# Sums of weight quarters on VectorE alone, and filters in half the steps

## The chip, the cores and the metric

The kernel runs on one core of one Trainium2 chip. It is one layer of a diffusion transformer in fp32, launched once. The metric is the device time of a launch in microseconds (us). Five engines work side by side: TensorE (PE: matrix products), VectorE (DVE), ScalarE (ACT), GpSimd (POOL) and SyncE (SP), which issues most of the DMAs. Each engine carries out its own instructions in the order of its own queue.

## The reference, cut to what matters

```python
def swiglu(x, wg, wu, wd):
    return (jax.nn.silu(x @ wg) * (x @ wu)) @ wd

def half_ffn(h, shift, scale, gate, wg, wu, wd):
    return h + 0.5 * gate * swiglu(modulate(rms_norm(h), shift, scale), wg, wu, wd)

def hyena_kernels(l, w1, b1, fr1, w2, b2, fr2, w3):
    t, z = hyena_pos_features(l)
    h = jnp.sin(fr1 * (z @ w1 + b1))
    h = jnp.sin(fr2 * (h @ w2 + b2))
    h = (h @ w3).astype(jnp.float32).reshape(l, HYENA_ORDER, 2, B_WIDTH)
    ...
    window = jnp.exp(-t[:, None] * deltas[None, :]) + HYENA_SHIFT
    h = h * window[:, None, None, :]
    kern = jnp.concatenate([h[:, :, 0], jnp.flip(h[:, :, 1], axis=0)], axis=0)
    return kern / (jnp.sum(jnp.abs(kern), axis=0, keepdims=True) + HYENA_L1_EPS)

def reference(x, c, ctx, ...):
    m = jnp.split((jax.nn.silu(c) @ mod_w[l] + mod_b[l])[:, None, :], N_MOD, axis=-1)
    ...
    h = half_ffn(h, m[0], m[1], m[2], ffn_w_gate[l, 0], ffn_w_up[l, 0], ffn_w_down[l, 0])
    hc = half_ffn(hc, mc[0], mc[1], mc[2], ffn_w_gate[l, 0], ffn_w_up[l, 0], ffn_w_down[l, 0])
    ...                    # norms, then the mixers: four gated recurrent heads and a Hyena convolution
    out, _, _ = token_mixers(n, s_fw, s_bw, hyena_kernels(n_lat, *filt_w), *mix_w)
    h = h + m[5] * out
    h = half_ffn(h, m[6], m[7], m[8], ffn_w_gate[l, 1], ffn_w_up[l, 1], ffn_w_down[l, 1])
    return rms_norm(h) * final_norm_w
```

The model width is 1024, with 512 tokens in `h`, 256 in the context `hc`, and 2816 hidden units (22 tiles of 128). The change lies in the first `half_ffn` and in `hyena_kernels`.

## The kernel before

Every fp32 product is made of three products of rounded parts. `split` (L141) casts a tile to its high part on ScalarE (L142) and subtracts that from the tile for the low part on VectorE or GpSimd (L143); `mm3` (L312) then issues the three products (L314, L315, L317).

The first feed-forward block treats 512 + 256 tokens and goes through the 22 hidden tiles in five groups: `GROUPS0` is 0-4, 4-8, 8-12, 12-16 and 16-22. Group 0 is made plainly. In the others (below: groups 1 to 4; the first three have four pairs of weight tiles, the last has six) two neighbouring tiles of `wg`, or of `wu`, are multiplied together in `pair_products0` (L869) by the seven products of the Strassen-Winograd scheme. With a pair's weight quarters a11, a12 (from the first tile, `src0`) and a21, a22 (from the second, `src1`), the seven left operands are p1: a11, p6: s2 = a11 + a21 + a22, p7: s3 = a11 + a21, p5: s1 = a21 + a22, p2: a12, p4: a22, p3: s4 = a12 + s2 (the weights are stored with the signs that make all of these additions). Each product is 12 matmuls of 386 columns. After each group but the last there follow the "down" products with `wd`; their sums go to DRAM through accumulating DMAs on GpSimd's queue (`y_dram`, `yc_dram`).

`quads0` (L239) prepares a pair's operands, one with each `yield`. a11, a12 and a22 are loaded as quarters into tiles `wraw`. s1 and s3 are made in tiles `qs` by two DMAs each: one of SyncE loads a quarter, one of GpSimd (L247) adds the other quarter to it. s2 and s4 are sums of VectorE (L254). a11, a12 and a22 are split with the subtraction on GpSimd, the others with VectorE. The ring of `wraw` tiles has three buffers of 128x1024, that of the split weights three as well; `weights(3)` keeps up to four or five operands ahead.

Between the products, `adv(bg)` moves on a background of other work: `mod_steps` (L393) loads a 128x1024 tile `wmod` of the modulation weights per step, into one of two buffers, and VectorE multiplies it by the conditioning vector and sums it up (L390: two `junk` products and one `wmod` product per tile for the first tiles, one for the later ones).

After the block come the residual and norms, then the input projections (`w_in`), beside which `filters` (L721) makes the Hyena filters in four passes (two channel halves, two orders). A pass is a generator whose `yield` hands a pair of estimated costs (TensorE, VectorE) to the class `Clock`, which decides when the next step is issued, and fills the time between steps with weight products. A pass has these steps: loads of the last weights `w3r` and of the first window (a decay table `win`); the weights' split into `w3h` and `w3l`; four steps, each with two taps products, the windowed product `hw` (L761) on VectorE, its sum and difference `pm` on GpSimd, and the next window's load; the norm; its reciprocal; six steps of the spectrum (`ps_k`). So twelve `yield`s follow the first two. The windows and `w3h`, `w3l` are tiles of the class `c2` (14 buffers of 512 columns).

The tiles `res` (`quarters`, two buffers of 128x2x770) hold the results of the pair products and, later, the gates of the recurrent heads (work items "z" of the table `todo`, L171). One weight of the last group's down products is kept there as well (`RES2`, L159); `ONE8` is a tile of another class, of 2080 columns, with twelve buffers.

What sets the order: the program is written as straight code with generators; a scheduler then places instructions on each engine's queue by a timeline of its own. SyncE's queue is in order: a load that waits for its buffer holds up the loads behind it.

## Time and profile before

| | |
|---|---|
| median of 3 runs | 1643.78 us (1643.22 to 1647.12) |
| profiled execution | 1642.22 us, span 1640.4 us, mean granted clock 0.953 |
| TensorE busy | 1489.6 us (91%) |
| VectorE busy | 1151.7 us (70%) |
| ScalarE, GpSimd busy | 631.7 us (39%), 467.8 us (29%) |
| groups 1 to 4 of the first block | 148.6-226.4, 259.9-347.8, 381.3-469.1, 502.5-621.3 us |
| the down products between them | 33.4 to 33.5 us each |
| filters, beside the norms and projections | from about 626 to 900 us |

The times are from one profiled execution, counted from the start of its span. A stretch in which TensorE is busy all the time at full clock (1.00, 2.4 GHz) has no room but by having less to multiply; a stretch with idle TensorE or a lower granted clock (0.5 is 1.2 GHz) does. The shares of the whole span average over stages that differ much, so the stretches are read one by one.

### The profile page before, as it was taken

The numbers are of one execution on the slowest core, as the hardware profiler recorded it, in microseconds if no ns is written. First come the engines' busy times: TensorE is split into PE (matmuls) and PEld (weight loads), VectorE is DVE, ScalarE is ACT, GpSimd is POOL, SyncE is SP. The second block draws the span as 40 slices with busy tenths as digits, with TensorE's granted clock in tenths as the row PEclk, the third lists the DMA queues.
The fourth block names the chain that finished last, engine by engine and source line by source line (L and its number), as shares of the span: only waits on it lengthen the run. The fifth ranks groups of instructions, "written<-read, shape, count | busy, mean of one in ns | idle before, by whom it ended". The sixth has DMA issues, their size and how long they took to land.

```text
span 1640.4 us, 22788 instructions
## 1 busy us (share of the span) xinstructions
PE 1489.6 (91%) x8560; PEld 1328.0 (81%) x8560; DVE 1151.7 (70%) x1811; ACT 631.7 (39%) x1133; POOL 467.8 (29%) x380
## 2 busy tenths in 40 slices
PE   8798897896896999989999998998789999999997
PEld 5687886886886887867778887887679899989897
DVE  7785784674774667866646986867566767969687
ACT  5253332332332443434323342344433443525353
POOL 1021443534534541332565001211332011202120
PEclk9899998998998999989999998999989999999999
DMA  9217559558568348243543443113343123333322
GB/s 388 88 59 247 164 151 233 141 151 224 145 170 204 90 107 307 81 147 110 170 150 105 135 167 135 65 52 116 103 149 110 50 73 109 104 103 96 112 76 91
DMA packets 95055, 224.57 MB, mean 137 GB/s; under 512 B 10651, under 2 KB 23711, under 8 KB 94304
## 3 DMA queue, kind: packets, MB, share of 16 engines
q1 hardware_dynamic: 79920, 198.69, 36.4%
q0 software_dynamic: 13440, 23.21, 8.0%
q8 instruction: 67, 1.10, 0.3%
q10 hardware_dynamic: 1584, 1.20, 0.2%
q14 instruction: 44, 0.36, 0.1%
HBM read 190.83 MB, written 32.24 MB: 136 GB/s over the span
## 4 chain that ended last, share of the span: by engine, by line
PE 60%; DMA 14%; DVE 12%; issue 7%; POOL 4%; ACT 3%; SPq 1%; ACTq 0%; POOLq 0%; DVEq 0%
DMA qs<-in_wg 5%; PE ps_w L314 5%; PE ps_w L317 5%; PE ps_w L315 5%; PE ps_dl L314 4%; PE ps_p L314 4%; PE ps_p L317 4%; PE ps_dl L317 4%; PE ps_p L315 4%; PE ps_dl L315 4%; DMA wmod<-in_mod_w 4%; DMA qs<-in_wu 3%; DVE wlo L143 2%; PE ps_s L1370 1%; PE ps_gl L314 1%
## 5 line engine op out<-in xcount | busy, mean ns | idle before, releaser
L142 ACT CAST whi<-wraw 128x512 fp32r<-128x512 f32 (+2 forms) x191 | 154.5, 810 | 273.5 <-issue 72.3
L143 DVE TENSOR_TENSOR wlo<-wraw,whi 128x1024 fp32r<-128x1024 f32 (+2 forms) x118 | 126.8, 1077 | 61.5 <-ACT whi L142 57.4
L317 PE MATMUL ps_w<-nhi,wlo 128*128 128x512 f32 x352 | 141.3, 402 | 6.8 <-DVE wlo L143 6.8
L314 PE MATMUL ps_w<-nhi,whi 128*128 128x512 f32 x352 | 144.5, 411 | 0.0
L315 PE MATMUL ps_w<-nlo,whi 128*128 128x512 f32 x352 | 141.0, 401 | 0.0
L317 PE MATMUL ps_dl<-mid,wlo 128*128 128x512 f32 (+1 forms) x330 | 128.4, 391 | 0.0
L315 PE MATMUL ps_dl<-mid,whi 128*128 128x512 f32 (+1 forms) x330 | 128.1, 389 | 0.0
L314 PE MATMUL ps_dl<-mid,whi 128*128 128x512 f32 (+1 forms) x330 | 126.8, 392 | 0.0
L143 POOL TENSOR_TENSOR wlo<-wraw,whi 128x1024 fp32r<-128x1024 f32 x19 | 47.2, 2485 | 248.4 <-ACT whi L142 244.2
L1570 POOL TENSOR_TENSOR u<-p,res 128x512 f32<-128x512 f32 x18 | 32.9, 1828 | 284.4 <-ACT p L1565 140.6
L390 DVE SCALAR_TENSOR_TENSOR wmod<-wmod,cvb 128x1024 f32<-128x1024 f32 x56 | 79.2, 1416 | 19.5 <-DMA wmod<-in_mod_w 19.1
L142 ACT CAST wlo<-qs 128x512 fp32r<-128x512 f32 x72 | 43.5, 618 | 113.1 <-DMA qs<-in_wu 45.1
L317 PEld LDWEIGHTS ps_w<-nhi,wlo 128*128 128x128 f32 x352 | 67.8, 193 | 20.7 <-DVE wlo L143 7.7
L314 PE MATMUL ps_p<-tt,wlo 128*128 128x386 f32 x72 | 31.1, 431 | 55.2 <-ACT wlo L142 55.2
L314 PEld LDWEIGHTS ps_w<-nhi,whi 128*128 128x128 f32 x352 | 68.1, 193 | 15.3
L142 ACT CAST whi<-qs 128x512 fp32r<-128x512 f32 x72 | 43.8, 619 | 93.8 <-DMA qs<-in_wg 34.9
L315 PEld LDWEIGHTS ps_w<-nlo,whi 128*128 128x128 f32 x352 | 68.2, 194 | 11.7
L143 DVE TENSOR_TENSOR wlo<-qs,wlo 128x512 fp32r<-128x512 f32 x72 | 63.1, 882 | 14.1 <-ACT wlo L142 13.8
L314 PEld LDWEIGHTS ps_dl<-mid,whi 128*128 128x128 f32 x330 | 62.5, 190 | 12.8 <-ACT mid L142 0.2
L254 DVE TENSOR_TENSOR qs<-qs,wraw 128x512 f32<-128x512 f32 x18 | 14.3, 796 | 82.1 <-DMA qs<-in_wg 61.9
L317 PEld LDWEIGHTS ps_dl<-mid,wlo 128*128 128x128 f32 x330 | 62.9, 191 | 8.2 <-DVE wlo L143 0.2
L315 PEld LDWEIGHTS ps_dl<-mid,whi 128*128 128x128 f32 x330 | 62.7, 190 | 7.9
(531 smaller groups left out, 4956.0 us busy)
## 6 DMA issues: line engine op xcount, KB each, us to landing
wmod<-in_mod_w SPq DMA_DIRECT2D x56, 512.0 KB, 4.0
wraw<-in_w_in SPq DMA_DIRECT2D x44, 512.0 KB, 3.5
wraw<-in_wd SPq DMA_DIRECT2D x37, 384.0 KB, 3.4
wraw<-in_wg SPq DMA_DIRECT2D x26, 512.0 KB, 4.0
wraw<-in_wu SPq DMA_DIRECT2D x26, 512.0 KB, 3.5
wraw<-in_wd SPq DMA_DIRECT2D x40, 256.0 KB, 3.0
wm<-in_mod_w SPq DMA_DIRECT2D x16, 512.0 KB, 10.0
wraw<-in_wg SPq DMA_DIRECT2D x27, 256.0 KB, 5.0
```

Source lines behind the costliest of these rows:

```text
L142: A.copy(hi, x)
L143: return eng.tensor_tensor(out=lo, in0=x, in1=hi.bitcast(F32), op=ALU.subtract)
L254: V.tensor_tensor(out=t, in0=x, in1=y, op=ALU.add)
L314: PE.matmul(o, whi, xhi, start=first, stop=False)
L315: PE.matmul(o, whi, xlo, start=False, stop=False)
L317: PE.matmul(o, wlo, xhi, start=False, stop=last)
L390: return V.scalar_tensor_tensor(out=out_, in0=raw, scalar=1.0, in1=vec, op0=ALU.mult, op1=ALU.mult, accum_out=res)
L1370: PE.matmul(p_[:, ss], km[:, ss], view(QA, c * P, ([2 * b, P // (2 * b)], [L + b, 2], [1, b])), start=True, stop=True)
L1570: G.tensor_tensor(out=u57, in0=p57, in1=res[:, 1:2].broadcast_to([P, 2, 256]), op=ALU.add)
```

## The change

Three things change. In `quads0` both tiles of a pair are loaded whole (512 KB each), and s1 and s3 are sums of VectorE, as s2 and s4 already were; the accumulating DMAs and the loads ahead of them are gone. In `filters` the windows and the split last weights lie in two `res` tiles, three windows are loaded at a pass's start and the fourth into the first one's place; the four steps of taps become two, with two products each, and the six of the spectrum two: after the first two `yield`s, six steps follow where there were twelve (2 for the taps, 1 for the norm, 1 for its reciprocal, 2 for the spectrum). The kept weight of the last group's down products goes to a tile of class `ONE8`, and the gates of head 0 are allowed only when all four passes are done.

```diff
--- before.py
+++ after.py
@@ -156,7 +156,7 @@
         else:
             plan += [(a[w][0, ft], a[w][0, ft + 1], QUAD0) for ft in range(f0, f1, 2) for w in ("wg", "wu")]
         down = [(a["wd"][0, dm, :, f0 * P:f1 * P], (f1 - f0) * P) for dm in range(KT)]
-        plan += hold(down, [RING] * 5 + [RES2] + [RING] * 2) + down[0:5] if g == len(GROUPS0) - 1 else down
+        plan += hold(down, [RING] * 5 + [ONE8] + [RING] * 2) + down[0:5] if g == len(GROUPS0) - 1 else down
     plan += [None] * 52
     plan += [(a["w_pa"][i], 1024) for i in range(4)]
     plan += hold([(a["w_out"][dm], 1024) for dm in range(KT)], [TWO4] * 4 + [ONE8] * 2 + [RING] * 2)
@@ -179,7 +179,7 @@
 
     def allowed(f):
         if f[0] == "z":
-            return f[1] == 0 or (state["conv"] and f[1] - state["heads"] < 3)
+            return (f[1] == 0 and "spectra" in state) or (state["conv"] and f[1] - state["heads"] < 3)
         if f[0] == "pb":
             return ("z", 3, 1) in state["done"] and state["heads"] > 1
         return True
@@ -238,16 +238,11 @@
 
     def quads0(src0, src1):
 
-        a11, a12 = raw_tile("wraw").rearrange("p (h c) -> h p c", h=2)
-        k0, k1 = slice(0, 512), slice(512, 1024)
-        load(a11, src0[:, k0])
-        s1, s3 = (c2("qs", [512]) for _ in range(2))
-        for t, x, y in ((s1, src1[:, k0], src1[:, k1]), (s3, src0[:, k0], src1[:, k0])):
-            load(t, x)
-            nc.gpsimd.dma_start(out=t, in_=y, accum_op=ALU.add)
-        load(a12, src0[:, k1])
-        a22 = raw_tile("wraw")[:, 0:512]
-        load(a22, src1[:, k1])
+        raws = []
+        for src in (src0, src1):
+            raws.append(raw_tile("wraw"))
+            load(raws[-1], src)
+        (a11, a12), (a21, a22) = (r.rearrange("p (h c) -> h p c", h=2) for r in raws)
 
         def total(x, y):
             t = c2("qs", [512])
@@ -262,9 +257,10 @@
             return t[:, 0], t[:, 1], None
 
         yield both(a11, G)
+        s1 = total(a21, a22)
         s2 = total(s1, a11)
         yield both(s2)
-        yield both(s3)
+        yield both(total(a11, a21))
         yield both(s1)
         yield both(a12, G)
         yield both(a22, G)
@@ -721,11 +717,6 @@
     def filters():
         worder = [(hh, q) for hh in range(2) for _ in range(2) for q in range(4)]
 
-        def window():
-            win = c2("win", [2, 256])
-            load(win, a["win"][worder.pop(0)])
-            return win
-
         for hh, o in ((0, 0), (0, 1), (1, 0), (1, 1)):
             cs = slice(hh * 256, hh * 256 + 256)
             raw = raw_tile("w3r")
@@ -736,9 +727,17 @@
             load(hyb, a["hy_bias"][o, cs].partition_broadcast(P))
             wl = mx.tile([1, 256], F32, tag="c1", name="wl", bufs=6)
             load(wl, a["win_last"][:, cs])
-            win = window()
+            third = lambda x, n: x.rearrange("p a b -> p (a b)")[:, 512 * n:512 * n + 512].rearrange("p (d c) -> p d c", d=2)
+            wins = quarters("win")
+
+            def window(n):
+                load(third(wins, n), a["win"][worder.pop(0)])
+                return third(wins, n)
+
+            win = [window(n) for n in range(3)]
             yield 0.0, 5.0
-            w3h, w3l = (c2(n, [2, 256], F32R) for n in ("w3h", "w3l"))
+            w3 = quarters("w3")
+            w3h, w3l = (third(w3, n).bitcast(F32R) for n in range(2))
             A.copy(w3h, w3r)
             V.tensor_tensor(out=w3l[0:64], in0=w3r[0:64], in1=w3h[0:64].bitcast(F32), op=ALU.subtract)
             V.tensor_scalar_mul(out=hyb, in0=hyb, scalar1=1.0 / 512.0)
@@ -753,14 +752,12 @@
                 PE.matmul(p_, h2s[:, j, t], w3h[:, d], start=True, stop=False)
                 PE.matmul(p_, h2s[0:64, j, t], w3l[0:64, d], start=False, stop=True)
 
-            for q in range(4):
-                p_ = ps("ps_w3")
-                taps(p_[:, 0:256], q, 0)
-                taps(p_[:, 256:512], q, 1)
+            def sample(q, p_):
+                nonlocal ab, late
                 hw = c2("hw", [2, 256])
-                V.tensor_tensor(out=hw, in0=p_.rearrange("p (d c) -> p d c", d=2), in1=win, op=ALU.mult)
-                if q < 3:
-                    win = window()
+                V.tensor_tensor(out=hw, in0=p_.rearrange("p (d c) -> p d c", d=2), in1=win[q], op=ALU.mult)
+                if q == 0:
+                    win.append(window(0))
                 pm = c2("pm", [2, 256])
                 G.tensor_tensor(out=pm[:, 0], in0=hw[:, 0], in1=hw[:, 1], op=ALU.add)
                 G.tensor_tensor(out=pm[:, 1], in0=hw[:, 0], in1=hw[:, 1], op=ALU.subtract)
@@ -769,10 +766,19 @@
                     ab = hw
                 else:
                     G.tensor_tensor(out=ab, in0=hw, in1=ab, op=ALU.add)
-                if late:
+                if late is not None:
                     split(ahi[:, :, q - 1], alo[:, :, q - 1], late)
                 late = pm
-                yield 0.45, 3.0
+
+            for q in (0, 2):
+                pq = []
+                for i in range(2):
+                    pq.append(ps("ps_w3"))
+                    taps(pq[i][:, 0:256], q + i, 0)
+                    taps(pq[i][:, 256:512], q + i, 1)
+                for i in range(2):
+                    sample(q + i, pq[i])
+                yield 0.9, 5.0
             G.tensor_tensor(out=ab[:, 0], in0=ab[:, 0], in1=ab[:, 1], op=ALU.add)
             pl = ps("ps_last")
             taps(pl[0:1, 0:256], 0, 1, last=True)
@@ -823,7 +829,11 @@
                     keep(2, tw[:, 1])
                     pool(fl(te[:, 1]), fl(te[:, 1]), fl(tw[:, 0]), ALU.subtract)
                     keep(3, te[:, 1])
-                yield 0.65, 0.0
+                if t is not to or k == 0:
+                    continue
+                yield 2.6, 0.0
+            yield 1.3, 0.0
+        state["spectra"] = True
 
 
     tsum = [None] * 4
```

How this moves instructions shows in the order of the queues. Three places follow. In the rows, numbers are positions in the queue, `L254` (before) and `L249` (after) are the sums of weight quarters, `L143` subtractions of splits, `L390` (after: `L386`) the modulation products, `L875`, `L882` (`L885`, `L892`) the takings of products from PSUM.

VectorE at the start of group 2, before; row 239 is the last instruction of the down stage:

```order
239 L390 SCALAR_TENSOR_TENSOR wmod,m_lat<-wmod,cvb 128x1024
240 L254 TENSOR_TENSOR qs<-qs,wraw 128x512
241 L254 TENSOR_TENSOR qs<-wraw,qs 128x512
242 L143 TENSOR_TENSOR wlo<-qs,wlo 128x512
243 L390 SCALAR_TENSOR_TENSOR junk,m_lat<-wmod,cvb 128x512
244 L143 TENSOR_TENSOR wlo<-qs,wlo 128x512
245 L390 SCALAR_TENSOR_TENSOR junk,m_part<-wmod,cvb 128x512
246 L143 TENSOR_TENSOR whi<-qs,whi 128x512
247 L390 SCALAR_TENSOR_TENSOR wmod,m_ctx<-wmod,cvb 128x1024
248 L143 TENSOR_TENSOR whi<-qs,whi 128x512
249 L875 TENSOR_TENSOR u_2368<-ps_p_2402,p_2367 128x385
```

VectorE at the same place now:

```order
242 L386 SCALAR_TENSOR_TENSOR wmod,m_lat<-wmod,cvb 128x1024
243 L249 TENSOR_TENSOR qs<-wraw 128x512
244 L249 TENSOR_TENSOR qs<-qs,wraw 128x512
245 L143 TENSOR_TENSOR wlo<-qs,wlo 128x512 x2
246 L386 SCALAR_TENSOR_TENSOR junk,m_lat<-wmod,cvb 128x512
247 L249 TENSOR_TENSOR qs<-wraw 128x512
248 L386 SCALAR_TENSOR_TENSOR junk,m_part<-wmod,cvb 128x512
249 L386 SCALAR_TENSOR_TENSOR wmod,m_ctx<-wmod,cvb 128x1024
250 L143 TENSOR_TENSOR whi<-qs,whi 128x512
251 L249 TENSOR_TENSOR qs<-wraw,qs 128x512
252 L885 TENSOR_TENSOR u_2351<-ps_p_2387,p_2350 128x385
253 L386 SCALAR_TENSOR_TENSOR wmod,m_lat<-wmod,cvb 128x1024
254 L143 TENSOR_TENSOR whi<-qs,whi 128x512
255 L249 TENSOR_TENSOR qs<-wraw 128x512
256 L249 TENSOR_TENSOR qs<-qs,wraw 128x512
257 L249 TENSOR_TENSOR qs<-wraw 128x512
258 L892 TENSOR_TENSOR g<-ps_p_2453,p_2350 128x385
```

The first two sums of the pair follow the modulation product directly in both; s3, now a sum too, stands behind a `junk` product. The first three sums of the second pair (rows 255 to 257) stand ahead of the last splits of the first pair (row 260).

SyncE's queue at the start of group 2, before:

```order
80 L136 DMA wraw<-in_wg 128x512 x2
81 L136 DMA wmod<-in_mod_w 128x1024
82 L136 DMA wraw<-in_wg 128x512
83 L136 DMA wmod<-in_mod_w 128x1024
84 L136 DMA wraw<-in_wu 128x512 x2
85 L136 DMA wmod<-in_mod_w 128x1024 x2
86 L136 DMA qs<-in_wg 128x512 x2
87 L136 DMA wraw<-in_wu 128x512
88 L136 DMA wraw<-in_wg 128x512 x2
89 L136 DMA wmod<-in_mod_w 128x1024
```

and now:

```order
77 L136 DMA wraw<-in_wg 128x1024
78 L136 DMA wmod<-in_mod_w 128x1024
79 L136 DMA wraw<-in_wg 128x1024
80 L136 DMA wmod<-in_mod_w 128x1024
81 L136 DMA wraw<-in_wu 128x1024
82 L136 DMA wmod<-in_mod_w 128x1024 x3
83 L136 DMA wraw<-in_wu 128x1024
84 L136 DMA wraw<-in_wg 128x1024
85 L136 DMA wmod<-in_mod_w 128x1024 x2
```

Each pair has two loads, without the loads into `qs`; the `wmod` loads keep their places between them.

VectorE at the start of group 4, before; row 429 is an instruction of the filters' first pass, which scales `hyb`:

```order
428 L390 SCALAR_TENSOR_TENSOR wmod,m_lat<-wmod,cvb 128x1024
429 L744 TENSOR_SCALAR hyb<-hyb 128x256
430 L254 TENSOR_TENSOR qs<-qs,wraw 128x512
431 L254 TENSOR_TENSOR qs<-wraw,qs 128x512
432 L143 TENSOR_TENSOR wlo<-qs,wlo 128x512
433 L390 SCALAR_TENSOR_TENSOR wmod,m_lat<-wmod,cvb 128x1024
434 L143 TENSOR_TENSOR wlo<-qs,wlo 128x512
435 L143 TENSOR_TENSOR whi<-qs,whi 128x512 x2
```

and now:

```order
439 L386 SCALAR_TENSOR_TENSOR wmod,m_lat<-wmod,cvb 128x1024
440 L249 TENSOR_TENSOR qs<-wraw 128x512
441 L249 TENSOR_TENSOR qs<-qs,wraw 128x512
442 L143 TENSOR_TENSOR wlo<-qs,wlo 128x512
443 L386 SCALAR_TENSOR_TENSOR wmod,m_lat<-wmod,cvb 128x1024
444 L143 TENSOR_TENSOR wlo<-qs,wlo 128x512
445 L249 TENSOR_TENSOR qs<-wraw 128x512
446 L249 TENSOR_TENSOR qs<-wraw,qs 128x512
447 L143 TENSOR_TENSOR whi<-qs,whi 128x512
448 L743 TENSOR_SCALAR hyb<-hyb 128x256
449 L143 TENSOR_TENSOR whi<-qs,whi 128x512
```

The instruction on `hyb` has moved from ahead of the first pair's sums to behind all four of them.

## Rows read from the trace of the kernel before

**Rows 1.** Page: the chain that ended last, shares of the span by engine.
```profile
PE 60%; DMA 14%; DVE 12%; issue 7%; POOL 4%; ACT 3%; SPq 1%; ACTq 0%; POOLq 0%; DVEq 0%
```
**Rows 2.** Windows: stretch, length, busy us (instructions) by engine, granted clock, DMA share, GB/s.
```profile
148.60:226.40 77.80, 63.92 (x339) 62.73 (x338) 57.20 (x86) 28.60 (x56) 37.24 (x31) 0.91 0.58 157
226.40:259.90 33.50, 33.50 (x193) 29.24 (x192) 22.89 (x51) 10.76 (x24) 13.42 (x15) 1.00 0.85 223
259.90:347.80 87.90, 67.84 (x339) 66.34 (x338) 55.62 (x86) 28.68 (x56) 39.37 (x33) 0.86 0.61 158
...
381.30:469.10 87.80, 64.92 (x339) 63.41 (x338) 57.46 (x88) 28.50 (x56) 39.96 (x33) 0.88 0.61 158
...
502.50:621.30 118.80, 100.10 (x511) 95.04 (x510) 69.83 (x100) 46.71 (x89) 56.34 (x49) 0.90 0.52 131
621.30:692.00 70.70, 67.34 (x370) 56.57 (x369) 54.76 (x83) 29.96 (x48) 15.38 (x15) 0.95 0.56 195
692.00:900.00 208.00, 199.50 (x918) 158.69 (x917) 129.38 (x154) 73.03 (x111) 94.48 (x88) 0.98 0.40 132
```
**Rows 3.** Timeline of TensorE, group 2: start, duration, line, what [idle before, releaser].
```profile
274.05 0.69 PE L314 MATMUL ps_p<-tt,wlo 128*128 128x386 f32 x1 [11.89 <-ACT wlo L142]
...
280.35 0.34 PE L317 MATMUL ps_p<-bh,wlo 128*128 128x386 f32 x1
...
291.63 0.33 PE L317 MATMUL ps_p<-bh,wlo 128*128 128x386 f32 x1
294.05 0.69 PE L314 MATMUL ps_p<-tt,whi 128*128 128x386 f32 x1 [2.09 <-ACT whi L142]
```
**Rows 4.** TensorE's waits, 148.6 to 621.3: total us, times, longest.
```profile
PE ps_p L314 <- ACT wlo L142: 55.2, 9, 12.9
PE ps_p L314 <- ACT whi L142: 20.0, 7, 5.0
```
**Rows 5.** Tiles qs, 148.6 to 621.3: durations ns min/median/max; who waited (us, times).
```profile
L143 DVE TENSOR_TENSOR wlo<-qs,wlo x36: 670/693/1783, 157.3 to 611.2; 128x512 fp32r<-128x512 f32 x36
...
L254 DVE TENSOR_TENSOR qs<-qs,wraw x18: 675/692/1308, 156.0 to 604.1; 128x512 f32<-128x512 f32 x18
...
  DVE qs L254: 82.1, 14
...
  PE ps_p L314: 75.3, 16
```
**Rows 6.** Chain of waits, 255 to 276: start, duration, what.
```profile
259.88 8.09 DMA qs<-in_wg
...
268.52 4.11 DMA qs<-in_wg
...
273.38 0.63 ACT wlo L142
```
**Rows 7.** Page, DMA issues: count, KB each, median us to landing.
```profile
wraw<-in_wg SPq DMA_DIRECT2D x26, 512.0 KB, 4.0
```
**Rows 8.** Page, costliest groups: count | busy us, mean ns | idle before.
```profile
L390 DVE SCALAR_TENSOR_TENSOR wmod<-wmod,cvb 128x1024 f32<-128x1024 f32 x56 | 79.2, 1416 | 19.5 <-DMA wmod<-in_mod_w 19.1
...
L254 DVE TENSOR_TENSOR qs<-qs,wraw 128x512 f32<-128x512 f32 x18 | 14.3, 796 | 82.1 <-DMA qs<-in_wg 61.9
```
**Rows 9.** SyncE's queue at group 2's start; DMA issues of the same stretch.
```profile
256.97 2.86 SPq L136 DMA_DIRECT2D wmod<-in_mod_w  x2
...
wmod<-in_mod_w SPq DMA_DIRECT2D x2, 512.0 KB, 7.0
```
**Rows 10.** Timeline of VectorE at the start of group 4.
```profile
512.51 0.29 DVE L744 TENSOR_SCALAR hyb<-hyb 128x256 f32<-128x256 f32 x1 [10.99 <-DMA hyb<-in_hy_bias]
```
**Rows 11.** Timelines of VectorE and GpSimd in group 2.
```profile
275.25 1.76 DVE L143 TENSOR_TENSOR wlo<-qs,wlo 128x512 fp32r<-128x512 f32 x1
...
275.12 1.34 POOL L143 TENSOR_TENSOR wlo<-wraw,wlo 128x512 fp32r<-128x512 f32 x1 [3.42 <-ACT wlo L142]
```
**Rows 12.** Waits in 621 to 900: us, times, longest.
```profile
POOL pm L765 <- DVE hw L761: 102.3, 15, 24.6
```

## Prediction

> **What bounds the kernel now.** I read the page first. The chain that ended last runs only 60% through TensorE: 14% of it is DMA and 12% VectorE [rows 1]. So somewhere TensorE waits for transfers, and the question is where. The table of windows answers it: the first feed-forward block has four groups of products with the "down" products between them, and of the two only the groups lose time. In the down stretch before the second group TensorE is busy 33.50 of 33.50 us at full clock; in the four groups it is busy 63.92 of 77.80, 67.84 of 87.90, 64.92 of 87.80 and 100.10 of 118.80 us, at a granted clock of 0.91, 0.86, 0.88 and 0.90 [rows 2]. Together the groups take 372.3 us.
>
> What the groups would take without waits comes from the timeline of TensorE. From the matmul at 280.35 to the one at 291.63 there are 64 steps in 11.28 us, 0.176 us each, at full clock (2.4 GHz); after the wait that ends at 274.05 it is 19 steps in 6.30 us, 0.33 each, the lower of its two levels [rows 3]. A pair of weight tiles gives 7 products of 12 matmuls: 84 x 0.176 = 14.8 us. Groups 1 to 3 have four pairs (59.1 us each), group 4 six (88.7): 266 us, so 106 us of the 372.3 are waits and low clock.
>
> Who is waited for: within the groups TensorE waits 55.2 us (9 times, up to 12.9) and 20.0 us (7 times) for ScalarE's casts of split weights [rows 4]. The casts are 0.63 us long [rows 6]; they are late because of what feeds them. The answer for the tiles `qs` (sums of weight quarters) names it: VectorE's second sum (L254) waited 82.1 us for these tiles' DMAs, and TensorE 75.3 [rows 5]. The chain at the start of group 2 shows how: VectorE has no more to do, the plain load of the first half takes 8.09 us from 259.88, only then can the accumulating DMA be issued by GpSimd (4.11 us), VectorE's sum follows, the cast starts at 273.38 and TensorE at 274.05, after 11.89 us of waiting [rows 3, 6]. So two transfers stand one behind the other in front of each sum.
>
> **The change part by part.** *The sums.* The 36 accumulating DMAs and the 36 loads ahead of them go; 54 loads of 256 KB become 36 of 512 KB, whose median landing in the same kernel is 4.0 us [rows 7], less than one of the two transfers of the pair. VectorE gets 36 more additions of 128x512. The existing ones, of the same shape and both inputs in SBUF, cost 796 ns on the mean, 692 in the median, 1308 at most [rows 5, 8]: I take 0.80. That is 8 x 0.80 = 6.4 us in each of groups 1 to 3 and 12 x 0.80 = 9.6 in group 4. VectorE's busy time becomes 57.2 + 6.4 = 63.6, 55.6 + 6.4 = 62.0, 57.5 + 6.4 = 63.9 and 69.8 + 9.6 = 79.4 [rows 2]. In the first three it is now above TensorE's 59.1: the bound passes to VectorE; in group 4 TensorE's 88.7 stays above.
>
> What is late next? (a) At a group's start the two first sums stand directly behind the last modulation product, and their raw tiles have landed during the down stage. But the next instruction, the first `junk` product, waits for its `wmod`, and the third sum stands behind it. SyncE issues that `wmod` between 256.97 and 259.83, as one of two, with a median landing of 7.0 us [rows 9]: about 258.4 + 7.0 = 265.4. Then 0.7 (`junk`) + 0.8 (sum) + 0.6 (cast) give 267.5, while TensorE has run p1 and p6 (2 x 2.1 us from 259.9) by 264.1: a wait of 3.4 us instead of 11.9. VectorE idles about 3 us there. The wait leaves the clock low: the 19 steps from 274.05 took 3 us more than at full clock (19 x 0.176 = 3.3) [rows 3]. (b) The first sum of the next pair stands in VectorE's row ahead of the present pair's last splits. Its raw tile can only be loaded into the slot that the present pair's fourth sum frees, and 2.1 us of VectorE's work (a modulation product, 1.42 on the mean [rows 8], and a subtraction, 0.69) lie between: 4.0 - 2.1 = 2 us of idleness per following pair, 3 x 2 = 6 in a group. If this reaches TensorE each time, it also loses clock: for a wait like that of 2.09 us before 294.05 [rows 3] I set half of those 3 us, 1.5.
>
> By VectorE a group is then 62 to 64 + 3 + 6 = 71 to 73; by TensorE 59.1 + 3.4 + 3 = 65.5 where the following pairs don't stall it, and 65.5 + 3 x 3.5 = 76 where each does. I take 72 for groups 1 to 3. For group 4 TensorE's 88.7 + 3.4 + 3 = 95. There `hyb` moves behind the sums: VectorE waited 10.99 us for it, until 512.51, ahead of its first sum [rows 10]; now p1, p6, p7 and p5 (8.4 us from 502.5, to 511) lie ahead of it. What this may cost is between 0 and those 11 us; I take 0, since the products before it nearly cover it. Sum: 3 x 72 + 95 = 311, against 372.3: **61 us less**.
>
> The Trainium skill ("SBUF — State Buffer", section "SBUF: two separate sides") speaks against adding such sums: a VectorE instruction with two SBUF inputs and a GpSimd instruction that reads SBUF exclude each other, and the second to start waits for the first one's whole length. The trace agrees in kind: the subtraction at 275.25 took 1.76 us on VectorE beside GpSimd's subtraction at 275.12, where its median is 0.69 [rows 5, 11]. By the mean of the rows this is in the 0.80 already, which gives the 1582 below; if the rule met every new sum, it would be the 1627 of the second rival.
>
> *GpSimd and the queues.* The 36 issues of the accumulating DMAs leave GpSimd's queue, which splits a11, a12 and a22. This may bring those splits forward; I count nothing, since the waits for `qs` make up all of TensorE's (75.3 of 55.2 + 20.0 [rows 4, 5]).
>
> *The kept down weight* changes its tile, with the same split: nothing, and no instruction more.
>
> *The filters.* The shorter form issues the same taps, products and additions; it makes two products at a time wait in PSUM, and asks for three windows at once. TensorE is idle for 3.4 us in 621.3 to 692 and 8.5 us in 692 to 900, its clock 0.95 and 0.98 [rows 2]: no more than 12 us of waiting and some 7 of clock can be gained there. GpSimd's waits for the windowed products (102.3 us) cost nothing as long as TensorE has other weights to multiply, and in this stretch it has [rows 2, 12]. The other end is the last rival. I take 0, with -15 to +15. That the first head's gates wait for the spectra puts nothing else in TensorE's rows behind the filters: 0.
>
> Sum: 1642.2 (the profiled execution) - 61 = 1581. The median of the runs is 1.6 us above the profiled execution, so 1582 is what I expect of the runs.
>
> **The rivals.** *TensorE alone is the bound.* VectorE's sums run in the down stages' slack (22.89 busy of 33.50 [rows 2]), nothing stalls: 266 for the groups, 1642 - 106 + 2 = 1538. For it: the raw tiles of two pairs can be loaded ahead. Against: three raw slots hold one pair and a half, and `wmod` still lands late.
>
> *VectorE and GpSimd exclude each other.* If each of the 24 new sums of groups 1 to 3, where VectorE is the bound, also meets a whole GpSimd subtraction (1.34 us [rows 11]), they cost 32 us more. In group 4 VectorE's path is 79.4 + 3 + 5 x 2 = 92.4 against TensorE's 95, so of 12 x 1.34 = 16 us there 13 count: 1582 + 45 = 1627. For it: maxima of 1308 among the present sums; against: their median of 692 [rows 5].
>
> *The raw slot decides.* The load into the freed slot lands as late as the plain load at 259.88 did, 8.09 us [rows 6], 6 us after VectorE comes to it instead of 2: 4 us more for each following pair, 3 x 3 x 4 = 36, and in group 4 5 x 4 = 20, of which 2.6 are slack (95 - 92.4): 36 + 17 = 53, 1635. For it: SyncE issues in order with `wmod` ahead. Against: the median of 4.0 [rows 7].
>
> *Slower: the filters hold up the weights.* A filter's windows and its last weights fill the two gates' tiles; the next filter's three windows stand in SyncE's row ahead of weights and are issued only when the first filter's last windowed product is made. The longest wait in the chain of these was 24.6 us [rows 12]; at each of three handovers TensorE could starve for as long, 3 x 24.6 = 74 us, more than the 61: 1656. It decides from 20 us at a handover on. Against: TensorE, which has other weights split ahead, waits just 8.5 us in all of 692 to 900, for all that these samples wait [rows 2, 12].
>
> *The sums' DMAs were hidden anyway*: no change, 1644. TensorE's 75 us of waits for them speak against it.
>
> **How the numbers follow.** Forecast 0.58 (its own range 1562 to 1602: -20 for the first three groups at 65.5, +20 for these at 76 and `hyb` at 8); TensorE alone 0.12; exclusion 0.13; raw slot 0.10; filters slower 0.05; nothing changes 0.02. A difference under 0.3% (5 us) can't be told from no change. Faster: 0.58 + 0.12 + 0.13 + 0.09 = 0.92; same 0.02 + 0.01 = 0.03; slower 0.05. The range from 1546 to 1630 leaves out the last two (0.07), most of the raw slot's case (0.07), the end of the exclusion's (0.02) and under half of TensorE's alone (0.05).
>
> **What would show it.** Right: the waits of TensorE for casts in the groups fall from 75 to 15 to 25 us, the groups take about 72, 72, 72 and 95, VectorE is busy for over 85% of the first three, the sums' mean stays below 0.9 us, and 621 to 900 keeps its length (279 us). Wrong: sums above 1.1 us on the mean (exclusion), a wait for `wraw` ahead of the first sum of each pair over 4 us (raw slot), waits of TensorE over 10 us beside the filters' windows, or groups that end within 62 us.

## The result and the profile after

The changed kernel takes 1572.42 us (median of 4 runs, 1569.79 to 1573.49) against 1645.2 of the kernel before in the same comparison: ratio 0.9555, 95% interval 0.9537 to 0.9574. The profiled execution took 1569.79 us with a span of 1568.0; the spans differ by 72.4 us. Here is where they went, by the stretches of the two traces (before, after):

| stretch | before | after | difference |
|---|---|---|---|
| groups 1, 2, 3, 4 | 77.6, 87.8, 87.6, 118.6 | 67.8, 72.3, 71.0, 95.7 | -64.8 |
| three down stages between them | 33.6 each | 34.3 each | +2.1 |
| end of group 4 to the spectra's end | 271.6 | 264.3 | -7.3 |
| the rest behind that | 747.7 | 745.4 | -2.3 |

Stretches run from the first matmul of a stage to the first of the next one. The table of windows of the changed kernel, to be laid beside [rows 2] (stretch, length, busy us and instructions of TensorE, its weight loads, VectorE, ScalarE, GpSimd, granted clock, DMA share, GB/s):

```profile
148.40:216.20 67.80, 62.14 (x338) 60.48 (x337) 60.92 (x85) 27.16 (x54) 34.34 (x23) 0.97 0.38 128
216.20:250.60 34.40, 34.13 (x194) 29.41 (x193) 23.49 (x54) 10.69 (x24) 13.89 (x16) 1.00 0.82 220
250.60:322.90 72.30, 63.89 (x338) 61.36 (x337) 65.61 (x91) 28.30 (x56) 36.05 (x25) 0.95 0.46 143
357.30:428.20 70.90, 63.17 (x338) 61.25 (x337) 64.06 (x91) 28.48 (x56) 34.63 (x25) 0.95 0.46 143
462.60:558.30 95.70, 93.06 (x510) 90.67 (x509) 79.39 (x108) 47.20 (x89) 49.39 (x38) 0.98 0.34 103
```

VectorE is now busy for 60.92 of 67.80, 65.61 of 72.30 and 64.06 of 70.90 us in groups 1 to 3: some 90%, where it was 63% to 74%. TensorE's waits in the groups answer to [rows 4] (total us, times, longest):

```profile
PE ps_p L310 <- ACT whi L142: 9.0, 5, 4.0
PE ps_p L313 <- DVE whi L143: 7.9, 4, 2.8
PE ps_p L313 <- DVE wlo L143: 5.0, 5, 1.1
PE ps_p L310 <- ACT wlo L142: 2.3, 2, 2.0
```

75.2 us have become 24.2, and half of them now name VectorE's subtractions. At the start of group 2, where TensorE waited 11.89 us [rows 3], the timeline of TensorE has two short waits, ahead of the second and of the third product:

```profile
254.84 0.44 PE L310 MATMUL ps_p<-tt,wlo 128*128 128x386 f32 x1 [1.96 <-ACT wlo L142]
...
260.43 0.44 PE L310 MATMUL ps_p<-tt,whi 128*128 128x386 f32 x1 [1.62 <-ACT whi L142]
```

What VectorE's time in the four groups and three down stages consists of (count | busy us, mean ns | idle before), after:

```profile
L386 DVE SCALAR_TENSOR_TENSOR wmod<-wmod,cvb 128x1024 f32<-128x1024 f32 x50 | 60.8, 1216 | 16.1 <-DMA wmod<-in_mod_w 15.7
L143 DVE TENSOR_TENSOR whi<-qs,whi 128x512 fp32r<-128x512 f32 x36 | 45.0, 1266 | 1.0 <-ACT whi L142 0.8
L249 DVE TENSOR_TENSOR qs<-wraw 128x512 f32<-128x512 f32 x35 | 36.8, 1051 | 10.2 <-DMA wraw<-in_wg 10.2
...
L249 DVE TENSOR_TENSOR qs<-qs,wraw 128x512 f32<-128x512 f32 x17 | 16.0, 943 | 0.5
L249 DVE TENSOR_TENSOR qs<-wraw,qs 128x512 f32<-128x512 f32 x18 | 13.5, 748 | 0.0
```

and two of the same groups before:

```profile
L390 DVE SCALAR_TENSOR_TENSOR wmod<-wmod,cvb 128x1024 f32<-128x1024 f32 x50 | 70.9, 1419 | 17.2 <-DMA wmod<-in_mod_w 16.8
...
L143 DVE TENSOR_TENSOR whi<-qs,whi 128x512 fp32r<-128x512 f32 x36 | 30.9, 871 | 4.7 <-ACT whi L142 4.7
```

A sum of two raw quarters costs 1051 ns, the old sums 943 and 748; the splits of `qs` went from 871 to 1266, while the modulation products fell from 1419 to 1216. The order on VectorE and GpSimd has shifted, and with it which instruction meets GpSimd's. The timelines of the two engines in group 2 of the changed kernel show it, VectorE first:

```profile
251.57 1.23 DVE L386 SCALAR_TENSOR_TENSOR wmod<-wmod,cvb 128x1024 f32<-128x1024 f32 x1 [1.93 <-DMA wmod<-in_mod_w]
...
252.72 0.69 DVE L249 TENSOR_TENSOR qs<-wraw 128x512 f32<-128x512 f32 x1
...
257.27 2.40 DVE L249 TENSOR_TENSOR qs<-wraw 128x512 f32<-128x512 f32 x1
...
261.46 1.77 DVE L143 TENSOR_TENSOR whi<-qs,whi 128x512 fp32r<-128x512 f32 x1
```
```profile
257.19 1.92 POOL L143 TENSOR_TENSOR wlo<-wraw,wlo 128x512 fp32r<-128x512 f32 x1
260.97 1.72 POOL L143 TENSOR_TENSOR whi<-wraw,whi 128x512 fp32r<-128x512 f32 x1 [1.86 <-ACT whi L142]
```

GpSimd's subtraction runs from 257.19 to 259.11, VectorE's sum starts at 257.27 and lasts until 259.67: 0.56 us after it, as if it had begun when the other ended; the same sum with no GpSimd instruction beside it takes 0.69 (252.72). At 260.97 and 261.46 it is the same, with 0.54 us. Of the 35 recorded sums of two raw quarters, the 17 that overlap no GpSimd computation take 0.67 to 0.69 us, the 18 others up to 2.49.

### The profile page after: what moved, and what is told of

Read it like the earlier page. It is cut to its first block, busy times and chain, and to the rows that moved or that the text cites. A ratio compares the mean times of both kernels' runs of the same rounds, so it can differ in the third digit from the quotient of the medians.

```text
span 1568.0 us, 22676 instructions
## 1 busy us (share of the span) xinstructions
PE 1474.8 (94%) x8560; PEld 1315.4 (84%) x8560; DVE 1194.0 (76%) x1847; ACT 631.2 (40%) x1133; POOL 454.1 (29%) x344
## 4 chain that ended last, share of the span: by engine, by line
PE 57%; DVE 23%; DMA 8%; issue 6%; ACT 3%; POOL 2%; SPq 0%; ACTq 0%; DVEq 0%; POOLq 0%
PE ps_w L310 5%; PE ps_w L313 5%; PE ps_w L311 5%; PE ps_p L313 4%; PE ps_p L310 4%; PE ps_p L311 4%; DMA wmod<-in_mod_w 3%; PE ps_dl L310 3%; PE ps_dl L313 3%; PE ps_dl L311 3%; DVE wlo L143 3%; DVE junk L386 2%; DVE qs L249 2%; DVE whi L143 2%; DMA wraw<-in_wd 2%
## 5 line engine op out<-in xcount | busy, mean ns | idle before, releaser
L143 DVE TENSOR_TENSOR wlo<-wraw,whi 128x1024 fp32r<-128x1024 f32 (+2 forms) x118 | 128.4, 1093 | 54.1 <-ACT whi L142 52.0
L143 POOL TENSOR_TENSOR wlo<-wraw,whi 128x1024 fp32r<-128x1024 f32 x19 | 51.7, 2722 | 244.8 <-ACT whi L142 237.1
L386 DVE SCALAR_TENSOR_TENSOR wmod<-wmod,cvb 128x1024 f32<-128x1024 f32 x56 | 69.0, 1234 | 18.8 <-DMA wmod<-in_mod_w 18.4
L313 PEld LDWEIGHTS ps_w<-nhi,wlo 128*128 128x128 f32 x352 | 66.3, 188 | 13.1
L143 DVE TENSOR_TENSOR wlo<-qs,wlo 128x512 fp32r<-128x512 f32 x72 | 64.2, 897 | 15.5 <-ACT wlo L142 14.6
L143 DVE TENSOR_TENSOR whi<-qs,whi 128x512 fp32r<-128x512 f32 x72 | 69.0, 972 | 3.5 <-ACT whi L142 3.4
L313 PEld LDWEIGHTS ps_dl<-mid,wlo 128*128 128x128 f32 x330 | 62.9, 191 | 8.8 <-DVE wlo L143 0.5
L313 PE MATMUL ps_p<-bh,whi 128*128 128x386 f32 x180 | 62.1, 345 | 6.6 <-DVE whi L143 6.6
```

Source lines behind the costliest of these rows:

```text
L143: return eng.tensor_tensor(out=lo, in0=x, in1=hi.bitcast(F32), op=ALU.subtract)
L313: PE.matmul(o, wlo, xhi, start=False, stop=last)
L386: return V.scalar_tensor_tensor(out=out_, in0=raw, scalar=1.0, in1=vec, op0=ALU.mult, op1=ALU.mult, accum_out=res)
```

## The experiments

All were timed against the kernel before; ratios are given with their 95% intervals. "Groups" are groups 1 to 4 in us, from the traces, to be compared with 371.6 before and 306.8 after.

**Only the sums.** `quads0` of the changed kernel in the kernel before:

```diff
-        load(a11, src0[:, k0])
-        s1, s3 = (c2("qs", [512]) for _ in range(2))
-        for t, x, y in ((s1, src1[:, k0], src1[:, k1]), (s3, src0[:, k0], src1[:, k0])):
-            load(t, x)
-            nc.gpsimd.dma_start(out=t, in_=y, accum_op=ALU.add)
...
+        s1 = total(a21, a22)
```

> Only the sums: quads0 of the changed kernel in the kernel before; filters, kept weight and gates as before. Theory (the series of two transfers ahead of each sum was the groups' cost, the filters give the small rest): the four groups take 300 to 312 us as in the changed kernel (306.8) instead of 371.6, the stretch from the last group's end to the spectra's end stays at 271 us as before (264 in the changed kernel), and the time is 1576 to 1586 us. Rival (the filters, or the tiles and the order they free, make a good part of the groups' gain): groups over 320, time over 1595.

Measured: 1582.04 us, ratio 0.9626 (0.9585 to 0.9667); groups 307.6; the stretch behind them 272.5. As the theory has it: the sums alone give what the groups gave, and nothing else.

**All but the sums** (`quads0` of before in the changed kernel, the reverse of the diff above).

> Everything but the sums: quads0 of before in the changed kernel. Theory: groups at about 372 us as before, the filters' stretch 7 us shorter, 1636 to 1642 us. Rival (the filters' stretch got shorter only because the groups ended otherwise, the shorter form itself is worth nothing): 1643 to 1648.

Measured: 1632.43 us, ratio 0.9927 (0.9900 to 0.9955); groups 369.1; the stretch behind them 267.1. So the filters' part is worth something by itself, 12 us by the runs and 6 by the spans. That is the theory's direction, but the stretch got 4.5 us shorter instead of 7, and the time lies below its 1636 to 1642.

**s1 on VectorE, s3 by two transfers again.**

```diff
+        s3 = c2("qs", [512])
+        load(s3, src0[:, 0:512])
+        nc.gpsimd.dma_start(out=s3, in_=src1[:, 0:512], accum_op=ALU.add)
...
-        yield both(total(a11, a21))
+        yield both(s3)
```

> Changed kernel, but s3 is made by a load and an accumulating DMA again, s1 stays on VectorE (18 sums fewer there). Theory A (a sum by two transfers comes late wherever its product stands early): p7, the third product, waits for s3 at each group's start and in the pairs, 8 us and more at four starts and 1 to 3 us per pair: 1595 to 1620. Theory B (VectorE is the groups' bound, and s3 is needed a product later than s2, so its transfers are hidden): 18 sums of 0.8 to 1.2 us less on the path, 1555 to 1567.

Measured: 1600.41 us, ratio 0.9736 (0.9702 to 0.9769); groups 333.5 (69.4, 78.8, 80.1, 105.2). TensorE's waits in them (total us, times, longest):

```profile
PE ps_p L313 <- ACT whi L142: 34.8, 6, 12.4
PE ps_p L316 <- DVE whi L143: 12.8, 7, 4.9
```

Theory A. The third product waits for s3 (7.67 us at the start of group 2), and a lighter VectorE does not help while a sum comes by two transfers.

**The new sums on GpSimd.**

```diff
-        s1 = total(a21, a22)
+        s1 = total(a21, a22, G)
...
-        yield both(total(a11, a21))
+        yield both(total(a11, a21, G))
```

(`total` takes the engine as a third argument.)

> Changed kernel, with the 36 new sums on GpSimd instead of VectorE. Theory A (VectorE's own load bounds groups 1 to 3, at 60.9 to 65.6 us busy): VectorE loses 8 sums of about 1.1 us per group, 8 to 9 us less in each of three groups, 1548 to 1560. Theory B (VectorE and GpSimd hold each other up when both have their inputs in SBUF, so moving an addition to the slower engine only makes its overlap longer, 1.34 us each and behind a11's split): groups of 70 to 85 us, 1572 to 1610.

Measured: 1582.82 us, ratio 0.9626 (0.9594 to 0.9658); groups 314.1 (67.4, 76.2, 73.6, 96.8). VectorE, with eight sums fewer, is busy just as long in group 2 (65.86 us for 65.61). There (count | busy us, mean ns), where the modulation product took 1213 in the changed kernel:

```profile
L386 DVE SCALAR_TENSOR_TENSOR wmod<-wmod,cvb 128x1024 f32<-128x1024 f32 x9 | 16.5, 1839 | 2.0 <-DMA wmod<-in_mod_w 1.9
L386 DVE SCALAR_TENSOR_TENSOR junk<-wmod,cvb 128x512 f32<-128x512 f32 x9 | 11.0, 1219 | 0.0
...
L249 DVE TENSOR_TENSOR qs<-qs,wraw 128x512 f32<-128x512 f32 x4 | 5.1, 1285 | 6.2 <-POOL qs L249 6.2
```
```profile
252.50:328.80 76.30, 65.49 (x339) 63.06 (x338) 65.86 (x83) 28.32 (x56) 47.55 (x34) 0.93 0.44 138
```

What VectorE saved, it lost again on the instructions that met more of GpSimd's, and it waited 6.2 us for sums of the slower engine: theory B.

**The other splits on VectorE too.** The reverse step: GpSimd no longer reads the raw tiles.

```diff
-        yield both(a11, G)
+        yield both(a11)
...
-        yield both(a12, G)
-        yield both(a22, G)
+        yield both(a12)
+        yield both(a22)
```

> Changed kernel with the splits of a11, a12, a22 on VectorE instead of GpSimd: 12 subtractions more for VectorE in each of groups 1 to 3, 0.69 us each where nothing disturbs it, 8.3 us. Theory A (VectorE's instructions of 1.2 to 1.4 us are those that GpSimd's subtractions hold up): without them they take 0.69, some 14 us less in a group, so groups of 62 to 68 and 1550 to 1567. Theory B (they are long for another reason): groups of 78 to 82, 1595 to 1610.

Measured: 1541.9 us, ratio 0.9402 (0.9385 to 0.9419), clear of the changed kernel's 0.9537 to 0.9574: faster than both kernels. Groups 280.3 (60.6, 63.4, 62.9, 93.4). VectorE has 12 subtractions more in a group and yet less to do; group 2 in its windows, and its instructions in the whole stretch (count | busy us, mean ns):

```profile
242.00:305.40 63.40, 60.59 (x338) 58.98 (x337) 60.85 (x104) 28.45 (x56) 17.86 (x14) 1.00 0.54 167
```
```profile
L249 DVE TENSOR_TENSOR qs<-wraw 128x512 f32<-128x512 f32 x35 | 32.7, 935 | 0.4 <-DMA wraw<-in_wg 0.2 <-DMA wraw<-in_wu 0.2
...
L143 DVE TENSOR_TENSOR whi<-qs,whi 128x512 fp32r<-128x512 f32 x36 | 29.0, 821 | 0.3 <-PE ps_p L313 0.2
...
L143 DVE TENSOR_TENSOR whi<-wraw,whi 128x512 fp32r<-128x512 f32 x26 | 20.2, 776 | 3.6 <-ACT whi L142 3.6
L143 DVE TENSOR_TENSOR wlo<-wraw,wlo 128x512 fp32r<-128x512 f32 x27 | 19.2, 710 | 0.0
```

The splits of `qs` are back at 821 (1266), the sums at 935 (1051); the moved subtractions cost 776 and 710 ns on VectorE. On GpSimd, in group 2 of the changed kernel, they took:

```profile
L143 POOL TENSOR_TENSOR wlo<-wraw,wlo 128x512 fp32r<-128x512 f32 x6 | 10.6, 1760 | 13.8 <-ACT wlo L142 13.8
L143 POOL TENSOR_TENSOR whi<-wraw,whi 128x512 fp32r<-128x512 f32 x5 | 8.6, 1722 | 7.4 <-DVE wmod L386 5.5 <-ACT whi L142 1.9
```

VectorE is busy for 60.85 us instead of 65.61, with 13 instructions more. Theory A, and faster than its 1550. The sums that still take 1.3 to 1.4 us in group 2 run beside GpSimd's remaining instructions of 1.0 to 1.5 us. One thing more changes: VectorE's waits for raw tiles fall from 10.2 us to 0.4. How much of the gain comes from tiles that are free earlier, and how much from shorter instructions, this run does not separate.

**The same splits in the kernel before** (the diff above applied to its `quads0`).

> Kernel before with the splits of a11, a12, a22 on VectorE, the accumulating DMAs as they were. Theory A (the groups of before waited for two transfers in series, and the mutual hold-up of VectorE and GpSimd was hidden behind that): groups of 365 to 375 us together, 1635 to 1645. Theory B (that hold-up was half of the groups' cost already before): groups under 345, below 1620.

Measured: 1639.86 us, ratio 0.9976 (0.9957 to 0.9995); groups 367.6. Theory A: as long as the sums came by transfers, the hold-up between VectorE and GpSimd lay behind those waits and hardly showed; it became a cost when they went.

**Modulation products cut short.** They take 64 columns, so the vectors are incomplete:

```diff
-                dot(r, r, cvb[1], m_ctx[:, col:col + 1])
+                dot(r[:, 0:64], r[:, 0:64], cvb[1][:, 0:64], m_ctx[:, col:col + 1])
```

(the other two products likewise).

> Changed kernel; the modulation products (L386) take 64 of their 512 or 1024 columns, so the modulation vectors are incomplete; all loads of wmod stay. VectorE loses some 16 to 18 us of 60.9 to 65.6 in each of groups 1 to 3. Theory A (VectorE's load bounds groups 1 to 3): they fall from 67.8, 72.3, 71.0 to 61 to 65 each, group 4 from 95.7 to 90 to 93; 1545 to 1555 us. Theory B (arrivals bind, of wmod at the start and of the raw tiles): groups shorter by 2 us at most, 1565 to 1573.

Measured: 1534.6 us, ratio 0.9353 (0.9328 to 0.9379); groups 59.2, 59.2, 59.2, 91.3, in which no wait of TensorE is left:

```profile
243.20:302.40 59.20, 59.20 (x338) 59.20 (x337) 47.24 (x88) 27.05 (x54) 30.61 (x25) 1.00 0.52 162
...
429.00:520.30 91.30, 91.30 (x510) 89.23 (x509) 76.88 (x105) 44.23 (x86) 50.22 (x37) 1.00 0.31 92
```

VectorE at 47 us of 59 no longer bounds anything. That this went under the range of theory A shows the floor: 59.2 + 59.2 + 59.2 + 91.3 = 268.9 us.

**A third buffer for `wmod`**, of class `c8`, with loads two steps ahead:

```diff
-        raw = [c4("wmod", [1024]) for _ in range(2)]
+        raw = [c4("wmod", [1024]) for _ in range(2)] + [c8("wmod", [1024])]
```

> Changed kernel with a third buffer for wmod, loaded two steps ahead. VectorE's waits for wmod (18.0 + 15.7 us in 148 to 558) should mostly go. Theory A (they are on the path at each start): 2 to 3 us less at each of four starts, 1560 to 1567. Theory B (VectorE has enough other work in its queue, or the load only moves into the raw loads' way): 1570 to 1577.

Measured: 1649.34 us, ratio 1.0056 (1.0038 to 1.0074): neither theory. The groups run at their floor (59.2, 59.2, 59.2, 93.1), but 133 us pass between group 4 and the first later weight product, in which TensorE has 17.8 us to do; its wait there (total us, times, longest), and what VectorE does in the stretch:

```profile
PE ps_dl L310 <- ACT mid L142: 110.9, 2, 100.1
```
```profile
L386 DVE SCALAR_TENSOR_TENSOR wmod<-wmod,cvb 128x1024 f32<-128x1024 f32 x53 | 64.1, 1223 | 15.9 <-DMA wmod<-in_mod_w 15.1
L386 DVE SCALAR_TENSOR_TENSOR junk<-wmod,cvb 128x512 f32<-128x512 f32 x46 | 31.7, 690 | 13.7 <-DMA wmod<-in_mod_w 12.9
```

The modulation work of the groups has slid behind them as a whole, 53 of the 56 products, one load after the other. SyncE issues five loads of `wmod` by 131.25 us and the next at 514.72. I read this as the added tile getting its buffer only there; that was not tried. It says nothing on the wait for `wmod`, but is a second case of groups without VectorE's modulation work.

**Half of the groups' modulation steps in the down stages**, in the changed kernel:

```diff
-        adv(bg)
+        adv(bg, 1 if group[0] == 4 else 0)
...
-                    adv(bg)
+                    adv(bg, 1 + (gi > 0 and dm % 2))
```

> Changed kernel with half of the modulation steps of groups 1 to 3 moved into the down stages behind them (12 steps there instead of 8, 4 in a group instead of 8). Theory A (VectorE bounds the groups and has slack in the down stages, 23.5 busy of 34.4): groups 5 us shorter each, down stages as before: 1556 to 1562. Theory B (the down stages take them at their own cost, by VectorE at 32 of 34 us or by the 2 MB more of transfers beside the accumulating ones, and the groups aren't VectorE's): 1569 to 1585.

Measured: 1565.08 us, ratio 0.9545 (0.9525 to 0.9565), against 0.9537 to 0.9574 of the changed kernel: no difference that can be told by ratios, and a time between the two theories. Groups 297.5 (60.9, 69.1, 68.9, 98.6). The gain of 6.9 in group 1 is theory A's; groups 2 and 3 gain 3.2 and 2.1, group 4 loses 2.9, and the stretch behind it is 3.8 longer (268.1).

**Both together**: splits on VectorE and modulation steps in the down stages. The text below calls both faster than the changed kernel; of the second that was not shown.

> The two versions that were faster than the changed kernel together: a11, a12, a22 split on VectorE, and half of the modulation steps of groups 1 to 3 in the down stages. Theory A (the groups are VectorE's, 57.8 to 61 us busy with the splits on VectorE; 4 steps fewer take 5 to 8 us off): groups of 59.2 to 60 us, TensorE's floor, in place of 60.6, 63.4, 62.9; the down stages 33.6 to 34.5; 1534 to 1540 us. Theory B (VectorE has no room left in the down stages, 23 to 24 busy of 33.6 and four steps more of some 2.2 us, or the loads collide there with the accumulating DMAs): down stages of 35 to 37, 1540 to 1550.

Measured: 1552.08 us, ratio 0.9438 (0.9415 to 0.9461): slower than the splits alone, a miss for both theories. Group 1 is at its floor, the down stages keep 33.7, but groups 2 to 4 take 65.1, 66.5, 96.5. VectorE's list for group 2 shows that the steps did not leave it:

```profile
L386 DVE SCALAR_TENSOR_TENSOR wmod<-wmod,cvb 128x1024 f32<-128x1024 f32 x9 | 11.9, 1335 | 0.0
L386 DVE SCALAR_TENSOR_TENSOR junk<-wmod,cvb 128x512 f32<-128x512 f32 x10 | 7.9, 787 | 4.0 <-DMA wmod<-in_mod_w 4.0
```

9 and 10 modulation products, where the changed kernel has 9 and 9 and the one with the splits alone 8 and 10. Only group 1 got rid of some (85 VectorE instructions there instead of 100): the order of the queues is made by the scheduler, not by the place of a call. Why the groups became longer than with the splits alone is open; VectorE is busy for 58.08 us in group 2 there and waits 4.0 for `wmod`.

**Twelve filter steps in the gates' tiles.** The changed kernel with the old loop:

```diff
-            for q in (0, 2):
...
-                yield 0.9, 5.0
+            for q in range(4):
+                p_ = ps("ps_w3")
+                taps(p_[:, 0:256], q, 0)
+                taps(p_[:, 256:512], q, 1)
+                sample(q, p_)
+                yield 0.45, 3.0
```

(and a `yield 0.65, 0.0` behind each of the six products of the spectrum).

> Changed kernel with twelve filter steps again (four of the taps, six of the spectrum); windows and last weights stay in the gates' tiles. Theory A (the fewer steps shift weight products behind the filters, where TensorE waited): the stretch from group 4's end to the first product behind the spectra is 271 us again instead of 264, 1577 to 1583 us. Theory B (the tiles free buffers of the class c2, and this shortens the stretch): 263 to 266 us, 1570 to 1575.

Measured: 1578.52 us, ratio 0.9597 (0.9580 to 0.9614), slower than the changed kernel (0.9555) by 0.4%; the time is theory A's, the stretch, with 267.8 us, lies between the two. The waits of TensorE show what the steps do. Behind the spectra, in the convolutions, the kernel before and this one have one wait that the changed kernel has not (before, this one, and the longest of the changed kernel in that stretch):

```profile
PE ps_j L314 <- ACT ys L142: 8.1, 1, 8.1
```
```profile
PE ps_j L310 <- ACT ys L142: 8.1, 1, 8.1
```
```profile
PE ps_i L311 <- DVE ys L143: 1.7, 1, 1.7
```

With fewer steps, 54 fewer weight matmuls (`ps_w`) are placed at the start of the convolutions and 69 more in the part behind (102 and 266 before, 48 and 335 now; with the twelve steps 102 and 263), and these fill the 8.1 us in which TensorE waited for ScalarE. The filters' stretch itself has fewer matmuls: 1237 before, 1225 with the twelve steps and 1213 in the changed kernel, by the traces, with TensorE busy for 259.74, 256.47 and 253.52 us. That is theory A for the steps, with its cost at another place than I had put it: not a shorter filter, but weight products left over for where they are needed. But the steps are only half of it: 3.5 of the 7.3 us come with them (267.8 to 264.3), and the other 3.8 are there with the twelve steps already. Whether those are the tiles' is not settled: only the sums gives 0.9626 and this one 0.9597, with overlapping intervals.

## Why the prediction was right, and where it was not

**The bound before.** Right. Sums by two transfers in series made the groups long: taking both out gives -64 us (only the sums), putting one of them back costs 27 (306.8 to 333.5).

**The groups.** Forecast 72, 72, 72 and 95, measured 67.8, 72.3, 71.0 and 95.7: -64.8 for -61. Against the 268.9 us of the groups without waits, 24 are waits of TensorE and 13 its lower clock. **The bound passes to VectorE**: right, by the modulation products cut short, where the first three groups drop to 59.2 and no wait is left; TensorE's floor of 59.1 and 88.7, taken from 64 steps, was 59.2 and 91.3.

**The terms behind the 72.** The start's wait, put at 3.4 us ahead of the third product, is 1.96 + 1.62 = 3.6 in group 2, but that the sizes agree is luck. The first part, ahead of the second product, was not in the sum: the last modulation product of the down stage itself waited 1.93 us for its `wmod`, until 251.57, and the first two sums stand behind it. The second part is no longer than what GpSimd added to the sum of 2.40 us at 257.27. The other groups begin with 0.33, 0.38 + 4.03 and 2.64 us. The clock's loss, put at 3 us per start, is 1.8 to 4.7 in a whole group. VectorE's busy time came out near the forecast (63.6, 62.0, 63.9 and 79.4; measured 60.92, 65.61, 64.06 and 79.39), by luck again: in the lists above the splits `whi` cost 14 us more and the modulation product `wmod` 10 less. Two other terms were mis-sized and cancelled. The wait for the raw slot was put at 2 us per following pair, 28 in all; VectorE's wait for raw tiles is 10.2 us in five waits:

```profile
DVE junk L386 <- DMA wmod<-in_mod_w: 18.0, 7, 4.7
...
DVE qs L249 <- DMA wraw<-in_wg: 10.2, 5, 3.1
```

In its place stands the hold-up between VectorE and GpSimd, which I had at its old mean (0.80 per sum). The 72 new and old sums came to 0.95 on the mean (66.3 us for the 70 in the record), and the splits `whi` to 1266 instead of 871. The mark I had set for it, sums below 0.9, was therefore missed, though not by enough to reach 1627.

**The second rival was half right.** The Trainium skill ("SBUF — State Buffer", section "SBUF: two separate sides") has a VectorE instruction with two SBUF inputs and a GpSimd instruction that reads SBUF exclude each other, and the second to start wait for the whole of the first. The rows at 257.19 and 257.27 agree. By the recorded starts the order is not always so clear: in group 3 a split on VectorE starts at 362.19, 0.07 us ahead of GpSimd's (1.92 us), and still ends 0.56 us after it. With the splits on VectorE the groups got 26.5 us shorter (306.8 to 280.3), raw tiles on time included. I had let only new sums pay for a meeting; but in these runs it falls on splits (871 to 1266), sums and, with the new sums on GpSimd, modulation products (1213 to 1839) in turn. The argument that I had set against this rival, the sums' median of 692, was no argument: the median of the new sums is 691 too, and their mean 1051:

```profile
L249 DVE TENSOR_TENSOR qs<-wraw x35: 673/691/2492, 151.8 to 540.6; 128x512 f32<-128x512 f32 x35
```

**`hyb`** at 0: right; VectorE waits 1.5 us for it now, against 10.99 [rows 10].

**The filters** at 0, within -15 to +15: the term that failed, by 7 to 10 us, inside its bounds. I looked for the gain in the filters' stretch alone and did not ask which weight products would be left for the stage behind it, where TensorE waited 8.1 us. That explains the part of the steps, 3.5 us; what the rest comes from stays open. The statement that 621 to 900 keeps its length was wrong: 7.3 us less to the spectra's end. The rival of filters that hold up weights did not happen: TensorE's longest wait in that stretch is 4.6 us. That head 0's gates wait for the spectra was put at 0; taken out of the changed kernel, that rule leaves the queues of TensorE, VectorE and SyncE the same row for row, so here it changes nothing.

## What to carry to other kernels

An operand made by two transfers in series is worth a compute instruction where its product stands early; make it from tiles that are there anyway. When the transfer goes, look at which engine's list is then longest, and who shares its SBUF reads: here moving three splits from GpSimd to the engine that was already 90% busy gave another 1.6% (0.9402 against 0.9555), because VectorE's other instructions and its waits got shorter by more than the moved splits added. In a list of the instructions such meetings showed here as a mean well above the median. And where weight products fill idle time, a stage that uses fewer of them is worth what they save at the next one.

## What the runs showed of the hardware that was not expected

In the four groups and three down stages of the changed kernel, VectorE's 128x512 additions and subtractions with both inputs in SBUF take 0.67 to 0.69 us where no GpSimd computation overlaps them (90 of them), and up to 2.55 us where one does (90). Its takings of products from PSUM, with one input in SBUF, keep 0.54 to 0.56 us with or without one. A 128x512 subtraction takes GpSimd 1.7 us in the median (1.27 to 2.41); on VectorE the moved ones took 0.71 and 0.78 on the mean. With 36 additions moved from VectorE to GpSimd, VectorE's busy time in group 2 did not fall (65.61 to 65.86 us): its modulation products rose from 1213 to 1839 ns.
